# Laying the second memory's split and keys between other tiles, and four more seven-product tiles, in a decoder trunk on one core

## The chip, the cores and the metric

The kernel runs on one core of a Trainium2 chip. A core has a matrix engine (TensorE, PE in the profile, with its weight loads as PEld), a vector engine (VectorE, DVE), an activation engine (ScalarE, ACT), a general engine (GpSimd, POOL) and SyncE (SP), which here issues almost all DMAs. Each engine works through its own queue in order; engines wait for each other on semaphores. The metric is the time of one execution on the device in microseconds (us), as the median of several runs.

## The reference

The reference is a two-layer decoder trunk over 512 tokens of width 1024, all in float32:

```python
for layer in range(DEPTH):
    if layer % 2 == 0:
        x = x + even_mixer(rms_norm(x, ev_norm[j]), ...)   # pooling + latent attention
    else:
        x = x + odd_mixer(rms_norm(x, od_norm[j]), ...)    # conv, gates, linear scan
    x = x + mem_cross_attention(rms_norm(x, xa_norm_x[layer]), mem, xa_norm_mem[layer], ...)
    x = x + swiglu(rms_norm(x, ffn_norm[layer]), ffn_w_gate_up[layer], ffn_w_down[layer])
return rms_norm(x, final_norm)
```

The pieces that the change touches:

```python
def odd_mixer(h, ...):
    gate_branch, xb = jnp.split(h @ w_in, [LRU_WIDTH], axis=-1)
    xb = causal_depthwise_conv(xb, conv_w, conv_b)
    ...                                  # sigmoid gates r, i; a = exp(log_a); b = mult * (i * xb)
    _, hseq = lax.associative_scan(linear_scan_combine, (a, b), axis=1)
    return (jax.nn.gelu(gate_branch) * hseq) @ w_out

def mem_cross_attention(h, mem, norm_mem, w_q, w_kv, w_o):
    m = rms_norm(mem, norm_mem)          # 256 memory tokens
    k, v = jnp.split(m @ w_kv, 2, axis=-1)
    ...

def swiglu(h, w_gate_up, w_down):
    g, u = jnp.split(h @ w_gate_up, 2, axis=-1)
    return (jax.nn.silu(g) * u) @ w_down
```

## The kernel before, in words

**Layout and precision.** Activations lie transposed: 1024 features are eight tiles of 128 partitions, with the 512 tokens along the free axis. To keep float32 accuracy with a rounded matmul type, each operand is split into a high and a low part. ACT writes the high part (a rounding copy), DVE the difference. A product of two split operands takes three matmuls (`mm3`, L162 to L171: high times high, high times low, low times high). So a matmul row in the profile has the line L169, L170 or L171 wherever it is issued, and the name of the tile that it writes (`mm`, `att`, `s`, `tr`, the four pairs of result banks) tells the places apart. A split of an activation has the lines L156 and L157, or L159 and L160 where a gain is multiplied in.

**Weights** (`Weights.get`, L84) are loaded by SyncE into two buffers of up to 128 x 1024 (L93), and split by ACT (L101) and DVE (L102) into four buffers each for the high and the low part. All stages share these buffers, in the order in which their weights are called for.

**The FFN** (`ffn`, L762) has 22 hidden tiles, in parts of 4, 4, 4, 4 and 6. A plain tile (L863) makes gate and up products of 512 columns, 2 x 8 x 3 = 48 matmuls. A seven-product tile (`fast`, L811) treats the same 2 x 2 block product by the seven-product scheme: 7 x 4 x 3 = 84 matmuls of 256 columns. It needs sums of weight halves (`sa`, `sb`, DVE), its own splits (`sw_h`, `sw_l`), and combines the results on DVE. Its raw weights (`gr`, L815) and the combined activations (`ta`, `tb`) live in a pool that is open only for the FFN (`st`, L879). Each hidden tile is multiplied by Silu (L855 in a seven-product tile, L866 in a plain one) and split (`hidden`, L781). After each part but the last, the down projection of that part is run two output tiles at a time behind the hidden tiles of the next part (`todo`, L913). `FAST` (L36) says which hidden tiles take the seven-product form: its first entry is for the second FFN, its second for the first.

At the end of the first FFN, the last part's down projection gives eight output tiles (L925). Each is added to the residual (L278, DVE) and fed to the next norm: split with the next block's gain (L159, L160) and squared (`feed`, L259). After the second output tile `aside` is called (L927). It makes the memory's second copy, `mg`: eight tiles of 256 columns, each scaled and split (L365, so L159 on ACT and L160 on DVE).

At the end of the second FFN, the last part's down weights are kept whole for the tail (`tailh`, `taill`, L885), in a pool that opens where the seven-product pool was closed (L883), before the last part's six tiles.

**The recurrent block** (`odd`, L931). Four heads of convolution tiles (`conv_tile`, L966) and gate products (`odg`, L1015, banks `att`) feed Sigmoid and Tanh on ACT. Then come eight tiles of the Gelu branch (`gate_tile`, L1041): 24 matmuls of 512 columns in bank `mm`, read out by a DVE multiply (L1044). Then the keys of the second memory (`mem_keys`, L369): eight tiles, 24 matmuls of 256 columns each, same banks, read out by L378. Then the scan (L1025: Exp and Square on ACT, L1031, L1035 and the scan instruction L1036 on DVE, with Sqrt on ACT between). Then Gelu of the eight gate tiles, their product with the scan's result (L1057) and its split, and the output projection (`odout`).

**What sets the order.** The program is written in one order, but a planner (the tile framework) lays each engine's queue: among the instructions that its own model has ready, it takes those earlier in the program first. It runs what is ready ahead of what still waits, across block borders. `issue_after(ins)` pins what follows behind `ins` in that engine's queue.

Of the kernel before, what the change touches and what calls it, by code (L numbers as in the profile page):

```python
# [9 lines left out]
F32 = mybir.dt.float32  # L10
F32R = mybir.dt.float32r
BF16 = mybir.dt.bfloat16
I32 = mybir.dt.int32
AF = mybir.ActivationFunctionType
ALU = mybir.AluOpType
# [3 lines left out]
P = 128  # L19
T = 512  # L20
D = 1024
KD = D // P
# [10 lines left out]
DFF = 2816  # L33
NF = DFF // P
FFN_PARTS = (4, 4, 4, 4, 6)
FAST = range(5, 16), range(5, 22)  # L36
HT = T // 2
KH = KD // 2
WARM = 12
# [67 lines left out]
class Trunk:  # L107
# [45 lines left out]
    def split(self, src, hi, lo, scale=None):  # L153
        nc = self.nc
        if scale is None:
            nc.scalar.copy(hi, src)  # L156
            nc.vector.tensor_sub(lo, src, hi.bitcast(F32))  # L157
        else:
            nc.scalar.activation(hi, src, AF.Copy, scale=scale)  # L159
            nc.vector.scalar_tensor_tensor(lo, src, scale, hi.bitcast(F32), op0=ALU.mult, op1=ALU.subtract)  # L160

    def mm3(self, out, terms, begin=True, end=True, **kw):  # L162

# [180 lines left out]
            self.nc.sync.dma_start(t, self.ins["memT"][i * 2 * P:(i + 1) * 2 * P, :].rearrange("(m p) t -> p m t", p=P))  # L344
        return [t[:, i, :] for t in tiles for i in range(2)]

    def mem_gained(self, layer, pool, tag, keys=True):


        nc = self.nc  # L350
        mem = self.mem_load(keys)
        mg = pool.tile([P, 2, KD, MEM], F32R, name=self.nm("mg"), tag=tag)
        if self.Rmem is None:
            ssq = self.new_ssq()
            for m in range(KD):
                self.add_square(ssq, mem[m], m == 0)
            cols = self.rstd_cols((ssq, D, NMT, None), bank="mm")[0]
            self.rmem = self.cst.tile([P, NMT], F32, name="rmem", tag="rmem")
            nc.vector.tensor_copy(self.rmem, cols)
            ps = self.bcast(cols, NMT, bank="mm")  # L360
            self.Rmem = self.cst.tile([P, MEM], F32, name="Rmem", tag="Rmem")
            nc.scalar.copy(self.Rmem, ps[:, :MEM])
        res = []
        for m in range(KD):
            self.split(mem[m], mg[:, 0, m, :], mg[:, 1, m, :], scale=self.vec("xa_norm_mem", layer * KD + m))  # L365
            res.append((mg[:, 0, m, :], mg[:, 1, m, :]))
        return res

    def mem_keys(self, layer, mg, m0, m1, low=None):  # L369

# [391 lines left out]
    def ffn(self, layer, nrm, nxt_spec, aside=None):  # L762


        nc, ins, tc = self.nc, self.ins, self.tc
        xg, A = nrm["xg"], nrm["side"]
        B = 1 - A
        final = nxt_spec is None
# [5 lines left out]
        lo, hi = slice(0, HT), slice(HT, T)  # L774
        xn, TA, TB = [None] * KD, [], []

        def products(f, xs):
            pg = self.linear(Wg, (layer * NF + f) * 2, xs, bank="mm")
            return pg, self.linear(Wg, (layer * NF + f) * 2 + 1, xs, bank="att")

        def hidden(u):  # L781
            h, l = self.pair(A)
            self.split(u, h, l)
            return h, l
# [78 lines left out]
        def plain(f):  # L863
            pg, pu = products(f, xn)
            t, u = self.tmp("t0"), self.tmp("t1")
            nc.scalar.activation(t, pg, AF.Silu)  # L866
            nc.vector.tensor_mul(u, pu, t)
            return hidden(u)
# [8 lines left out]
        todo, f0, nxt = [], 0, None  # L877
        fastp = ExitStack()
        st = fastp.enter_context(self.tc.tile_pool(name=f"fast{layer}", bufs=1))  # L879
        for p, nf in enumerate(FFN_PARTS):  # L880
            last = p == len(FFN_PARTS) - 1
            if last and final:
                fastp.close()  # L883
                pool = self.ctx.enter_context(self.tc.tile_pool(name="tail", bufs=1))
                into = [pool.tile([P, KD, nf * P], F32R, name=f"tail{i}", tag=f"tail{i}") for i in "hl"]  # L885
                Wd = Weights(self, ins[f"ffn_down{p}"], f"dn{layer}_{p}", into=into)
            hs = []
            if p == 0:

                pg = self.linear(Wg, layer * NF * 2, xg, bank="mm")  # L890
                with tc.issue_after(self.mm_ins):
                    cols = self.rstd_cols((nrm["ssq"], D, NT, None))[0]
                with tc.issue_after(self.sum_ins):
                    ps = [(pg, self.linear(Wg, layer * NF * 2 + 1, xg, bank="att"))]
                with tc.issue_after(self.mm_ins):
                    row = self.bcast(cols)
                R = self.rp.tile([P, T], F32, name=self.nm("R"), tag="R")
                nc.scalar.copy(R, row)
                with tc.issue_after(self.row_ins):
                    ps.append(products(1, xg))  # L900
                for i, (pg, pu) in enumerate(ps):
                    t, u = self.tmp("t0"), self.tmp("t1")
                    nc.vector.tensor_mul(t, pg, R)
                    nc.scalar.activation(t, t, AF.Silu)
                    nc.vector.tensor_mul(u, pu, R)
                    nc.vector.tensor_mul(u, u, t)
                    if i == 0:
                        gs = normed(st)
                    hs.append(hidden(u))
                halves(st, gs)  # L910
            for f in range(f0 + len(hs), f0 + nf):
                hs.append(fast(f, st) if f in FAST[not final] else plain(f))
                for _ in range(2):  # L913
                    if todo:
                        m = KD - len(todo)
                        self.residual(m, todo.pop(0)())
            f0 += nf
            if not last:
                todo = down(p, hs)
        if final:  # L920
            self.tail(Wd, hs, layer * KD, B)
# [2 lines left out]
        nxt = self.next_norm(B, *nxt_spec)  # L924
        for m, run in enumerate(down(p, hs)):  # L925
            self.residual(m, run(), nxt)
            if m == 1 and aside:  # L927
                aside()
        return nxt

    def odd(self, nrm, nxt_spec):  # L931
        nc, ins, tc = self.nc, self.ins, self.tc
# [5 lines left out]
        with ExitStack() as ctx:  # L938
            pool = ctx.enter_context(tc.tile_pool(name="od", bufs=1))
# [101 lines left out]
            def gate_tile(m):  # L1041
                ps = self.linear(Win, m, xg)
                t = self.actp.tile([P, T], F32, name=self.nm("g"), tag=f"act{other}")
                nc.vector.tensor_mul(t, ps, self.Rrow)  # L1044
                return t
# [1 line left out]
            self.Rrow = self.norm_row(nrm["ssq"], D)  # L1047
            sums, row = self.sum_ins, self.row_ins
            lru_gates()
            gates = [gate_tile(m) for m in range(KD)]  # L1050
            self.mem_keys(1, self.mg, 0, KD, None)
            lru_scan()
            with run():
                for m, t in enumerate(gates):
# [83 lines left out]
@with_exitstack  # L1138
def tile_trunk(ctx: ExitStack, tc: tile.TileContext, ins, out):
    k = Trunk(ctx, tc, ins, out)  # L1140
    nrm = k.setup()
    nrm = k.even(nrm, ("xa_norm_x", 0))
    nrm = k.cross(0, nrm, ("ffn_norm", 0))
    with ExitStack() as kept:
        def ready():
            k.mg = k.mem_gained(1, kept.enter_context(tc.tile_pool(name="mg1", bufs=1)), "mg")

        nrm = k.ffn(0, nrm, ("od_norm", 0), ready)
        nrm = k.odd(nrm, ("xa_norm_x", KD))
        nrm = k.cross(1, nrm, ("ffn_norm", KD), k.mg)  # L1150
    k.ffn(1, nrm, None)
# [82 lines left out]
```

## Time and profile before

| | |
|---|---|
| median of 3 runs | 1397.79 us (1396.98 to 1399.87) |
| profiled execution, its own time | 1396.59 us |
| its span, first to last instruction | 1394.8 us |
| TensorE busy | 1359.9 us, 97% |
| weight loads busy | 1178.4 us, 84% |
| VectorE busy | 927.0 us, 66% |
| ScalarE busy | 655.1 us, 47% |
| GpSimd busy | 122.0 us, 9% |
| bytes read from memory | 135.93 MB |
| mean granted clock | 0.992 |

The profile is of one execution. A row of a group or of the order in time names the line of the kernel, the engine, the operation and its tiles as out<-in. Time in square brackets is how long the engine was idle before the instruction, with the one that released it. The granted clock is the share of full speed that the chip's throttle gave TensorE in that stretch. Matmuls overlap, so one matmul's duration is longer than the distance to the next.

### The profile page before, as it was taken

The page shows a single profiled execution, that of the slowest core. Times are in us where ns is not written, and L with a number is a line of the kernel's source. Part 1 is how long each engine was busy: PE and PEld are TensorE (multiplying, and loading weights), DVE is VectorE, ACT ScalarE, POOL GpSimd, SP SyncE. Part 2 cuts the span into 40 slices and gives each one's busy share as a digit, 9 for nine tenths or more (in the row PEclk, how much of TensorE's full clock was granted, in tenths as well). Part 3 has the DMA queues.
Part 4 walks back from the last instruction along what each step waited for, and adds up shares of the span by engine and source line. Part 5 has one row for each costly group of instructions (what it writes and reads, how often), then busy time and mean ns, then how long its engine had stood idle before and what let it go on. Part 6 is the DMA issues. An engine that isn't in the chain of part 4 may idle for free.

```text
span 1394.8 us, 19076 instructions
## 1 busy us (share of the span) xinstructions
PE 1359.9 (97%) x7496; PEld 1178.4 (84%) x7496; DVE 927.0 (66%) x1449; ACT 655.1 (47%) x1053; POOL 122.0 (9%) x131
## 2 busy tenths in 40 slices
PE   8989999999999999999899979999999999999997
PEld 7777788888889999999788868888888999998887
DVE  6787574455787777777778595435549777764443
ACT  6577653354444444444535664335435344443231
POOL 0441021013000000000110001211120000000001
PEclk9999999999999999999999999999999999999999
DMA  6331252223242323331322324222324223213231
GB/s 208 99 97 39 75 183 89 93 89 105 82 141 96 107 91 109 103 103 31 115 96 90 106 79 163 91 76 91 106 95 145 93 95 103 94 53 125 92 91 61
DMA packets 44970, 139.40 MB, mean 100 GB/s; under 512 B 5584, under 2 KB 9808, under 8 KB 44880
## 3 DMA queue, kind: packets, MB, share of 16 engines
q1 hardware_dynamic: 43440, 136.86, 30.2%
q8 instruction: 59, 0.97, 0.3%
q10 hardware_dynamic: 1440, 1.32, 0.3%
q14 instruction: 31, 0.25, 0.1%
HBM read 135.93 MB, written 2.10 MB: 99 GB/s over the span
## 4 chain that ended last, share of the span: by engine, by line
PE 87%; DVE 5%; ACT 3%; issue 2%; DMA 0%; POOL 0%; POOLq 0%; DVEq 0%; ACTq 0%
PE mm L169 14%; PE mm L170 14%; PE mm L171 14%; PE s L171 6%; PE s L170 6%; PE s L169 6%; PE att L169 6%; PE att L170 6%; PE att L171 6%; PE tr L170 1%; PE tr L171 1%; PE tr L169 1%; DVE xk_l L102 1%; DVE act L157 1%; PE att L680 1%
## 5 line engine op out<-in xcount | busy, mean ns | idle before, releaser
L169 PE MATMUL s<-act,dn_h 128*128 128x512 f32 x304 | 120.0, 395 | 3.2 <-ACT act L156 3.2
L170 PE MATMUL s<-act,dn_h 128*128 128x512 f32 x304 | 120.0, 395 | 0.6 <-DVE act L157 0.6
L171 PE MATMUL s<-act,dn_l 128*128 128x512 f32 x304 | 116.3, 396 | 0.0
L250 POOL TENSOR_TENSOR ssq<-ssq,t 128x512 f32<-128x512 f32 (+1 forms) x37 | 59.1, 1598 | 633.4 <-ACT t L249 633.1
L156 ACT CAST sw_h<-gr 128x1024 fp32r<-128x1024 f32 (+1 forms) x56 | 46.8, 835 | 92.9 <-PE att L170 52.6
L278 DVE TENSOR_TENSOR x<-s,x 128x512 f32<-128x512 f32 x72 | 49.6, 688 | 35.8 <-PE s L171 35.7
L101 ACT CAST gu_h<-gu_raw 128x1024 fp32r<-128x1024 f32 x32 | 33.7, 1053 | 83.5 <-PE mm L170 53.1
L169 PEld LDWEIGHTS s<-act,dn_h 128*128 128x128 f32 x304 | 57.8, 190 | 14.7 <-ACT act L156 3.7
L170 PEld LDWEIGHTS s<-act,dn_h 128*128 128x128 f32 x304 | 57.9, 190 | 11.7 <-DVE act L157 1.0
L171 PEld LDWEIGHTS s<-act,dn_l 128*128 128x128 f32 x304 | 57.9, 190 | 10.4
L157 DVE TENSOR_TENSOR sw_l<-gr,sw_h 128x1024 fp32r<-128x1024 f32 (+1 forms) x56 | 53.6, 957 | 14.8 <-ACT sw_h L156 12.1
L170 PE MATMUL mm<-tb,sw_h 128*128 128x256 f32 x224 | 63.4, 283 | 0.0
L171 PE MATMUL mm<-tb,sw_l 128*128 128x256 f32 x224 | 63.3, 283 | 0.0
L169 PE MATMUL mm<-tb,sw_h 128*128 128x256 f32 x224 | 62.8, 280 | 0.0
L101 ACT CAST dn_h<-dn_raw 128x1024 fp32r<-128x1024 f32 (+1 forms) x40 | 40.3, 1007 | 46.2 <-ACT pc L846 14.6
L156 ACT CAST sw_h<-sb 128x1024 fp32r<-128x1024 f32 x28 | 29.4, 1048 | 65.8 <-PE s L170 58.2
L102 DVE TENSOR_TENSOR dn_l<-dn_raw,dn_h 128x1024 fp32r<-128x1024 f32 (+1 forms) x40 | 46.8, 1171 | 14.5 <-ACT dn_h L101 14.1
L102 DVE TENSOR_TENSOR gu_l<-gu_raw,gu_h 128x1024 fp32r<-128x1024 f32 x32 | 39.2, 1224 | 23.3 <-ACT gu_h L101 23.2
L278 DVE TENSOR_TENSOR x<-mm,x 128x512 f32<-128x512 f32 x24 | 16.4, 691 | 51.7 <-PE mm L171 51.7
L169 PE MATMUL mm<-act,gu_h 128*128 128x512 f32 x128 | 50.6, 395 | 0.0
L171 PE MATMUL mm<-act,xq_l 128*128 128x512 f32 x128 | 50.1, 391 | 0.0
L169 PE MATMUL att<-act,gu_h 128*128 128x512 f32 x128 | 50.0, 390 | 0.0
(478 smaller groups left out, 4450.7 us busy)
## 6 DMA issues: line engine op xcount, KB each, us to landing
gr<-in_ffn_gu_dram SPq DMA_DIRECT2D x56, 512.0 KB, 3.5
gu_raw<-in_ffn_gu_dram SPq DMA_DIRECT2D x32, 512.0 KB, 3.5
dn_raw<-in_ffn_down_dram SPq DMA_DIRECT2D x32, 512.0 KB, 3.5
xk_raw<-in_xa_w_k_dram SPq DMA_DIRECT2D x16, 512.0 KB, 3.5
xq_raw<-in_xa_w_q_dram SPq DMA_DIRECT2D x16, 512.0 KB, 3.5
xv_raw<-in_xa_w_v_dram SPq DMA_DIRECT2D x16, 512.0 KB, 3.5
xo_raw<-in_xa_w_o_dram SPq DMA_DIRECT2D x16, 512.0 KB, 3.5
odin_raw<-in_od_w_in_dram SPq DMA_DIRECT2D x16, 512.0 KB, 3.5
```

The costliest lines, as they stand in the source:

```text
L101: nc.scalar.copy(hi, src)
L102: self.low.tensor_sub(lo, src, hi[:, :].bitcast(F32))
L156: nc.scalar.copy(hi, src)
L157: nc.vector.tensor_sub(lo, src, hi.bitcast(F32))
L169: nc.tensor.matmul(out, wh, xh, start=begin and i == 0, stop=False, **kw)
L170: nc.tensor.matmul(out, wh, xl, start=False, stop=False, **kw)
L171: self.mm_ins = nc.tensor.matmul(out, wl, xh, start=False, stop=end and i == last, **kw).ins
L250: (low or nc.gpsimd).tensor_add(ssq[:, :n], ssq[:, :n], sq[:, :n])
L278: self.nc.vector.tensor_add(self.x[m], ps, self.x[m] if src is None else src)
L680: nc.tensor.matmul(banks[t], a[:, ts], wh[:, ws], start=k == 0, stop=False)
```

## The change

Three edits. In the second FFN, hidden tiles 16 to 19 take the seven-product form; the seven-product pool is therefore closed, and the tail's pool opened, before tile 20 instead of before tile 16. The split of the memory's second copy is made in pieces, and after output tiles 1 to 7 of the first FFN one or two of them are queued behind that tile's own split, on ACT and on DVE. In the recurrent block, keys 0 to 3 follow gate tiles 0 to 3, and keys 4 to 7 follow gate tiles 4 to 7.

```diff
-FAST = range(5, 16), range(5, 22)
+FAST = range(5, 20), range(5, 22)
@@ def split
-            nc.scalar.copy(hi, src)
-            nc.vector.tensor_sub(lo, src, hi.bitcast(F32))
+            a = nc.scalar.copy(hi, src)
+            b = nc.vector.tensor_sub(lo, src, hi.bitcast(F32))
...
+        self.split_ins = a.ins, b.ins
@@ def mem_gained(..., later=False)
-        res = []
-        for m in range(KD):
+        def piece(m):
             self.split(mem[m], mg[:, 0, m, :], mg[:, 1, m, :], scale=self.vec("xa_norm_mem", layer * KD + m))
-            res.append((mg[:, 0, m, :], mg[:, 1, m, :]))
-        return res
+            return mg[:, 0, m, :], mg[:, 1, m, :]
+
+        return piece if later else [piece(m) for m in range(KD)]
@@ def ffn
-            last = p == len(FFN_PARTS) - 1
-            if last and final:
-                fastp.close()
-                pool = self.ctx.enter_context(self.tc.tile_pool(name="tail", bufs=1))
-                into = ...
-                Wd = ...
...
             for f in range(f0 + len(hs), f0 + nf):
+                if final and f == FAST[0].stop:
+                    fastp.close()
+                    pool = self.ctx.enter_context(tc.tile_pool(name="tail", bufs=1))
+                    into = ...
+                    Wd = ...
                 hs.append(fast(f, st) if f in FAST[not final] else plain(f))
...
         for m, run in enumerate(down(p, hs)):
             self.residual(m, run(), nxt)
-            if m == 1 and aside:
-                aside()
+            if aside:
+                a, b = self.split_ins
+                with tc.issue_after(a), tc.issue_after(b):
+                    aside(m)
@@ def odd
-            gates = [gate_tile(m) for m in range(KD)]
-            self.mem_keys(1, self.mg, 0, KD, None)
+            gates = []
+            for m in (0, KH):
+                gates += [gate_tile(i) for i in range(m, m + KH)]
+                self.mem_keys(1, self.mg, m, m + KH)
             lru_scan()
@@ def tile_trunk
-        def ready():
-            k.mg = k.mem_gained(1, kept.enter_context(tc.tile_pool(name="mg1", bufs=1)), "mg")
+        def ready(m):
+            if m == 0:
+                k.mg = []
+                k.piece = k.mem_gained(1, kept.enter_context(tc.tile_pool(name="mg1", bufs=1)), "mg", later=True)
+            k.mg += [k.piece(i) for i in ((), (0,), (1, 2), (3,), (4,), (5,), (6,), (7,))[m]]
```

More of the change, by code (lines that the diff above doesn't have):

```diff
@@ L155, in split @@
         if scale is None:
-            nc.scalar.copy(hi, src)
-            nc.vector.tensor_sub(lo, src, hi.bitcast(F32))
-        else:
-            nc.scalar.activation(hi, src, AF.Copy, scale=scale)
-            nc.vector.scalar_tensor_tensor(lo, src, scale, hi.bitcast(F32), op0=ALU.mult, op1=ALU.subtract)
+            a = nc.scalar.copy(hi, src)
+            b = nc.vector.tensor_sub(lo, src, hi.bitcast(F32))
+        else:
+            a = nc.scalar.activation(hi, src, AF.Copy, scale=scale)
+            b = nc.vector.scalar_tensor_tensor(lo, src, scale, hi.bitcast(F32), op0=ALU.mult, op1=ALU.subtract)
+        self.split_ins = a.ins, b.ins
     def mm3(self, out, terms, begin=True, end=True, **kw):
@@ L345, in mem_load, with mem_gained @@
         return [t[:, i, :] for t in tiles for i in range(2)]
-    def mem_gained(self, layer, pool, tag, keys=True):
+    def mem_gained(self, layer, pool, tag, keys=True, later=False):
         nc = self.nc
@@ L880, in ffn @@
         for p, nf in enumerate(FFN_PARTS):
-            last = p == len(FFN_PARTS) - 1
-            if last and final:
-                fastp.close()
-                pool = self.ctx.enter_context(self.tc.tile_pool(name="tail", bufs=1))
-                into = [pool.tile([P, KD, nf * P], F32R, name=f"tail{i}", tag=f"tail{i}") for i in "hl"]
-                Wd = Weights(self, ins[f"ffn_down{p}"], f"dn{layer}_{p}", into=into)
             hs = []
@@ L911, in ffn @@
             for f in range(f0 + len(hs), f0 + nf):
+                if final and f == FAST[0].stop:
+                    fastp.close()
+                    pool = self.ctx.enter_context(tc.tile_pool(name="tail", bufs=1))
+                    into = [pool.tile([P, KD, nf * P], F32R, name=f"tail{i}", tag=f"tail{i}") for i in "hl"]
+                    Wd = Weights(self, ins[f"ffn_down{p}"], f"dn{layer}_{p}", into=into)
                 hs.append(fast(f, st) if f in FAST[not final] else plain(f))
@@ L917, in ffn @@
             f0 += nf
-            if not last:
+            if f0 < NF:
                 todo = down(p, hs)
```

## The prediction

> **What bounds the kernel now.** I read the page first, then the waits of TensorE, then the busy time of the engines in chosen stretches, and last the instructions in order of time around the two places that these views point to.
>
> ```profile
> span 1394.8 us, 19076 instructions
> PE 1359.9 (97%) x7496; PEld 1178.4 (84%) x7496; DVE 927.0 (66%) x1449; ACT 655.1 (47%) x1053; POOL 122.0 (9%) x131
> ```
>
> TensorE (PE) bounds the kernel: it is idle for 35 us of 1394.8. So there are two ways to gain: fewer matmuls, or less of those 35 us. The profiled execution took 1396.59 us, 1.8 more than its span, and lies 1.2 below the median of 1397.79; every sum below is taken from 1396.59, and 1.2 is added for the median.
>
> Waits of PE over the whole span; the columns are total us, times, longest:
>
> ```profile
> PE mm L169 <- DVE g L1044: 6.8, 2, 6.2
> PE s L169 <- ACT act L156: 3.2, 1, 3.2
> ...
> PE mm L169 <- DVE keys L378: 0.8, 1, 0.8
> ...
> PE s L170 <- DVE act L157: 0.6, 1, 0.6
> ```
>
> Two places hold most of it: the end of the first FFN (3.2 + 0.6) and the gates and keys of the recurrent block (6.8 + 0.8). The change touches both. Busy time by stretch (length, then PE, PEld, DVE, ACT, POOL, then the granted clock):
>
> ```profile
> 675.81:682.64 6.83, 6.39 (x14) 4.65 (x15) 6.40 (x16) 4.65 (x8) 1.38 (x1) 0.50 0.31 73
> ...
> 819.60:822.59 2.99, 0.06 (x1) 0.00 (x0) 2.99 (x5) 2.14 (x4) 0.00 (x0) 1.00 0.24 99
> 822.59:829.41 6.82, 3.52 (x16) 3.55 (x17) 6.82 (x11) 4.01 (x7) 0.00 (x0) 0.50 0.12 34
> 829.41:834.25 4.84, 4.03 (x35) 3.86 (x33) 4.84 (x9) 1.67 (x2) 0.00 (x0) 1.00 0.49 173
> 834.25:848.70 14.45, 14.45 (x120) 14.45 (x121) 10.40 (x18) 7.49 (x12) 0.00 (x0) 1.00 0.51 161
> ...
> 805.00:820.00 15.00, 14.07 (x72) 11.35 (x70) 15.00 (x19) 9.91 (x15) 0.00 (x0) 1.00 0.30 98
> ```
>
> After each of the two waits the granted clock is 0.50 for 6.8 us. The busy matmul time inside counts half: 6.39 / 2 = 3.2 us are lost at the first place, 3.52 / 2 = 1.8 at the second. So the first place costs 3.2 + 0.6 + 3.2 = 7.0 us, the second 6.8 + 0.8 + 1.8 = 9.4. Note also that VectorE (DVE) has no idle time at all from 805 to 834.25: in that stage it, not PE, sets the pace.
>
> **Part one: four more seven-product tiles (f = 16 to 19 of the second FFN).** A plain tile issues 48 matmuls of 512 columns, a seven-product tile 84 of 256. Each tile calls Silu once, so the distance between two Silus is the time of one tile with its two output tiles. L855 is the seven-product tile, L866 the plain one; the last two rows are the last product's read-out at today's boundary and the first cast into the tail's weights:
>
> ```profile
> 1241.29 0.63 ACT L855 ACTIVATE t<-t 128x512 f32<-128x512 f32 x1
> ...
> 1256.87 0.63 ACT L855 ACTIVATE t<-t 128x512 f32<-128x512 f32 x1
> ...
> 1302.38 0.59 ACT L866 ACTIVATE t<-mm 128x512 f32<-128x512 f32 x1
> ...
> 1318.70 0.59 ACT L866 ACTIVATE t<-mm 128x512 f32<-128x512 f32 x1
> ...
> 1328.48 0.84 ACT L101 CAST tailh<-dn_raw 128x768 fp32r<-128x768 f32 x1 [3.70 <-DMA dn_raw<-in_ffn_down_dram]
> ```
> ```profile
> 1265.07 0.42 DVE L859 SCALAR_TENSOR_TENSOR t<-mm,t 128x256 f32<-128x256 f32 x1 [0.90 <-PE mm L171]
> ```
>
> 15.58 against 16.32: 0.74 us per tile, **3.0 us** for four. The extra work (sums of weights, smaller casts, two combinations per tile) falls on DVE and ScalarE (ACT), and PE covers it:
>
> ```profile
> 1120.00:1155.00 35.00, 35.00 (x243) 32.69 (x242) 27.33 (x38) 14.94 (x21) 0.00 (x0) 1.00 0.29 99
> ...
> 1295.00:1330.00 35.00, 35.00 (x156) 28.97 (x156) 13.87 (x16) 9.91 (x12) 0.00 (x0) 1.00 0.29 97
> ```
>
> In the seven-product stage DVE is at 27.33 of 35 and PE still at 35.00; were that cover gone, DVE's 12 us per tile would be the next bound, still under 15.58. The eight weight loads of these tiles move from the two-buffer weight pool to the tiles' own buffers. What moves later is the opening of the tail's weight space, which lies where the seven-product tiles' buffers were. Today the last such tile reads out 8.2 us after its Silu (1265.07 - 1256.87); four tiles on, that is 1256.87 + 4 x 15.58 + 8.2 = 1327.4, and the tail's first cast is at 1328.48 already. So it is hidden by 1 us, and behind that by the two plain tiles that stay. Bounds: 0 if the casts come late enough to cost it all, 3.0 as measured. I take 3.0.
>
> **Part two: the memory's split laid among the first FFN's output tiles.** ACT, then DVE, in order of time:
>
> ```profile
> 670.25 0.84 ACT L101 CAST dn_h<-dn_raw 128x768 fp32r<-128x768 f32 x1 [5.32 <-PE mm L170]
> 670.99 3.30 ACT L159 ACTIVATE mg<-keys,vecs 128x256 fp32r<-128x256 f32 x8
> ...
> 674.29 0.60 ACT L156 CAST act<-t 128x512 fp32r<-128x512 f32 x1
> 674.91 1.28 ACT L950 ACT_TABLE_LOAD   x1
> ```
> ```profile
> 671.12 0.96 DVE L102 TENSOR_TENSOR dn_l<-dn_raw,dn_h 128x768 fp32r<-128x768 f32 x1
> ...
> 672.33 3.25 DVE L160 SCALAR_TENSOR_TENSOR mg<-keys,vecs,mg 128x256 fp32r<-128x256 f32 x8
> 675.49 0.69 DVE L157 TENSOR_TENSOR act<-t,act 128x512 fp32r<-128x512 f32 x1
> ...
> 677.09 0.17 DVE L954 TENSOR_TENSOR sp_z<-sp_z 128x8 f32<-128x8 f32 x1
> ```
>
> The split of the last hidden tile, for which PE waits, stands in both queues behind all eight pieces of the memory: 3.2 us on each engine. Pinned behind the output tiles' own splits, the pieces can no longer get ahead of it. ACT's cast then starts near 671.1 and DVE's difference near 675.49 - 3.16 = 672.3. What is late next is that difference: PE's second product waits until about 673, some 0.9 us, and the first output tiles' read-out perhaps 0.6 more. Of 7.0 us, 1.5 stay: a gain of **5.5**, if the clock keeps up. The rows ask for about 3 us of idle before a drop (2.99 before 822.59, 3.2 here); 1 to 1.5 us is well under.
>
> [...]
>
> The pieces themselves: one per output tile (0.49 on ACT, 0.48 on DVE). One output tile on DVE:
>
> ```profile
> 692.90 0.69 DVE L278 TENSOR_TENSOR x<-s,x 128x512 f32<-128x512 f32 x1 [1.81 <-PE s L171]
> 693.76 1.23 DVE L102 TENSOR_TENSOR odin_l<-odin_raw,odin_h 128x1024 fp32r<-128x1024 f32 x1 [0.17 <-ACT odin_h L101]
> 694.90 0.75 DVE L160 SCALAR_TENSOR_TENSOR act<-x,vecs,act 128x512 fp32r<-128x512 f32 x1
> ```
>
> 2.7 of some 4 us, so half a microsecond more costs nothing; what queues behind a piece is the next tile's weight split, which is early. The memory's own load is not on this path:
>
> ```profile
> L344 SPq DMA_DIRECT2D keys<-in_memT_dram x8: 379/448/680, 8.2 to 180.6; - x8
> ```
>
> Its last transfer is issued at 180.6. Bounds: 0 to 7.0; a loss is excluded, since nothing new is put ahead of the split.
>
> **Part three: four key tiles between the gate tiles.** Nothing is added or removed; eight gate tiles (24 matmuls of 512) and eight key tiles (24 of 256) change order, and with them the weight loads on SyncE's queue and their splits. DVE, with two rows of PE:
>
> ```profile
> 805.36 1.20 DVE L102 TENSOR_TENSOR xk_l<-xk_raw,xk_h 128x1024 fp32r<-128x1024 f32 x1
> ...
> 815.79 0.66 DVE L1044 TENSOR_TENSOR g<-mm,R 128x512 f32<-128x512 f32 x1
> ...
> 825.08 0.67 DVE L1044 TENSOR_TENSOR g<-mm,R 128x512 f32<-128x512 f32 x1
> ...
> 826.26 1.22 DVE L102 TENSOR_TENSOR xk_l<-xk_raw,xk_h 128x1024 fp32r<-128x1024 f32 x1
> ...
> 835.48 0.68 DVE L157 TENSOR_TENSOR act<-h,act 128x512 fp32r<-128x512 f32 x1
> ...
> 839.85 1.23 DVE L102 TENSOR_TENSOR xk_l<-xk_raw,xk_h 128x1024 fp32r<-128x1024 f32 x1 [1.21 <-ACT xk_h L101]
> ```
> ```profile
> 816.16 0.39 PE L171 MATMUL mm<-act,odin_l 128*128 128x512 f32 x1
> ...
> 848.71 0.40 PE L169 MATMUL mm<-act,odout_h 128*128 128x512 f32 x1
> ```
>
> The last gate tile's matmuls end at 816.55, its read-out comes at 825.08: 8.5 us in DVE's queue behind the scan. It holds one of two banks, so PE waits. The eight key weights are ready between 806.6 and 841.1, one per 4.9 us, because their splits stand in the same queue; a key tile needs only 24 x 14.45 / 120 = 2.9 us of PE. In the new order the first four keys use weights that are split before 800, where gate weights are split today, and the late slots serve gates 4 to 7 (24 x 35 / 156 = 5.4 us of PE each, more than 4.9) and keys 4 to 7. DVE's work is the same, so its last slot, 841.1, stays; key 7 follows with 2.9 us and the output projection starts at 844.0 instead of 848.71: 4.7. As the gate tiles now arrive later, DVE has fewer of their products to do around 820 and the slots come a little sooner: I take **5.0**. Bounds: 9.4 if PE never waits; on the other side, if each of four key tiles is read out 8.5 us late, two banks make one tile per (2.9 + 8.5) / 2 = 5.7 us, 2.8 more than now, 11.2 in all, with 3.2 for a clock drop: 9.4 - 14.4, a loss of 5.
>
> **Sum:** 3.0 + 5.5 + 5.0 = 13.5; 1396.59 - 13.5 + 1.2 = 1384.3, say **1384**.
>
> **Rivals.** *A: the FFN stall is refilled.* With the pieces gone, ACT's table load (1.28) and DVE's row of some twenty small instructions (0.17 to 0.2 each, 4 us) may slip ahead of the hidden tile's split as the pieces did. For: they already stand directly behind it. Against: they depend on one another and on the table, so they become ready one by one. Then 1 of 5.5 is left: gain 9.0, 1389.
>
> *B: DVE keeps the odd stage.* It is busy without a gap there, no work is taken from it, and the instruction order in its queue is the planner's; if the halves come out in an order that leaves PE waiting as long as now, part three gives 0: gain 8.5, 1389. That the change does not do what it says (the keys still queued behind all gates) gives the same. A and B together leave 4: 1394.
>
> *C: slower.* Gate 7 moves from before the keys to their middle. Its way to the output projection (read-out, Gelu, product, split) took from 816.55 to 836.16, 20 us. Its weight is now ready at 827.5, its matmuls end at 832.9, and after the same 20 us its product is there at 853. The projection starts at 844 and can run 21 of 24 matmuls of two tiles without it, 42 x 0.224 = 9.4 us, to 853.4: just covered. From 20.5 us on, each microsecond costs one, and 3.2 more for the clock; the gain is eaten at 31 us. If each of the three DVE steps waits as long again, 40 us, PE waits 19.5 + 3.2 and the time is 1384 + 22.7 = 1407. For: the queue is saturated. Against: DVE's backlog ends near 841.
>
> **Chances.** Forecast 0.48, A 0.15, B 0.20, both 0.07, C 0.10. The likeliest alone spans 1379 to 1388, just short of A and B. The range for 8 in 10 runs from 1377 (3.0 + 7.0 + 9.4 = 19.4, the whole of both places, and 1.4 for the spread of the runs) to 1396, which takes in A, B and both; C lies outside. A measurement of this kernel can tell about 0.2%, 2.8 us: faster takes forecast, A, B and part of both, 0.80; same 0.09; slower 0.11.
>
> **What would show it.** Silus of f = 16 to 19 at 15.6 us (part one), and the tail's first matmul without a wait. No group of eight pieces before the last hidden split, PE's wait there near 1 us, granted clock 1.00 through 675 to 683 (part two). PE's wait for the gate read-out under 2 us in total, clock 1.00 around 822, the output projection starting 4 to 5 us sooner relative to the start of the stage (part three). Wrong if PE waits for small instructions of the next block (A), for key or gate read-outs as long as now (B), or in the projection for the last product (C).

## The result, and the profile after

The changed kernel takes **1384.64 us** (1382.47 to 1386.88) where the kernel before, timed beside it, takes 1398.49 (1396.98 to 1399.87): a ratio of 0.9906, 95% interval 0.9892 to 0.9920. In a second session it took 1386.82 beside 1397.67, ratio 0.9917 (0.9899 to 0.9936). Its profiled execution took 1385.45 us, 11.1 less than the one before. The head of its page:

```profile
span 1383.7 us, 19425 instructions
...
PE 1353.7 (98%) x7640; PEld 1180.2 (85%) x7640; DVE 951.2 (69%) x1489; ACT 665.8 (48%) x1073; POOL 121.9 (9%) x131
```

TensorE (PE) is busy for 6.2 us less and idle for 30 us in place of 35. PE's waits at the two places, from the waits of the whole span and of the stretch around the first FFN's end (total us, times, longest):

```profile
PE mm L170 <- DVE g L1046: 2.8, 1, 2.8
...
PE mm L170 <- DVE keys L379: 2.3, 2, 1.6
...
PE s L171 <- DVE act L157: 0.6, 1, 0.6
PE s L170 <- DVE x L279: 0.5, 1, 0.5
```

The code's lines have moved by a few: the gate read-out is L1046, the keys' L379, the product L1061, the matmuls L170 to L172. The stall at the FFN's end is down to 0.6 + 0.5. Of 7.6 us at the gates and keys, 5.1 are left. Where the time went is read from starts in the order of time. The changed kernel:

```profile
670.05 0.28 PE L172 MATMUL mm<-tb,sw_l 128*128 128x256 f32 x1
...
704.79 0.39 PE L187 MATMUL tr<-ones,ssq 128*128 128x1 f32 x3
...
782.90 1.28 ACT L987 ACT_TABLE_LOAD   x1
...
840.47 0.39 PE L170 MATMUL mm<-act,odout_h 128*128 128x512 f32 x1
...
1339.21 0.34 PE L170 MATMUL mm<-act,tailh 128*128 128x384 f32 x1
```

The kernel before:

```profile
670.05 0.28 PE L171 MATMUL mm<-tb,sw_l 128*128 128x256 f32 x1
...
710.38 0.50 PE L186 MATMUL tr<-ones,ssq 128*128 128x1 f32 x4
...
788.49 1.28 ACT L985 ACT_TABLE_LOAD   x1
...
1350.37 0.34 PE L169 MATMUL mm<-act,tailh 128*128 128x384 f32 x1
```

The five rows are the last seven-product matmul of the first FFN, the sum for the next norm, the scan's first table load, the output projection (848.71 before) and the tail. Up to 670.05 the two traces take the same time. The distances to the next row hold one part each: 34.74 against 40.33 us at the end of the FFN (part two, 5.6), 57.57 against 60.22 from the table load to the projection (part three, 2.65), 498.74 against 501.66 from there to the tail (part one, 2.9). From the norm's sum to the table load both take 78.11.

Part one, in ScalarE's (ACT) order; the four new seven-product tiles lie between the first two rows:

```profile
1248.65 0.62 ACT L856 ACTIVATE t<-t 128x512 f32<-128x512 f32 x1
...
1310.99 0.63 ACT L856 ACTIVATE t<-t 128x512 f32<-128x512 f32 x1
1321.41 0.84 ACT L101 CAST tailh<-dn_raw 128x768 fp32r<-128x768 f32 x1 [0.77 <-DMA dn_raw<-in_ffn_down_dram]
```

The distance is 62.34 / 4 = 15.585 us per tile. Part two, first ACT, then VectorE (DVE), with the clock behind it (length; busy time of PE, PEld, DVE, ACT, POOL; granted clock):

```profile
671.11 0.60 ACT L156 CAST act<-t 128x512 fp32r<-128x512 f32 x1
671.73 1.28 ACT L952 ACT_TABLE_LOAD   x1
...
672.34 0.68 DVE L157 TENSOR_TENSOR act<-t,act 128x512 fp32r<-128x512 f32 x1
```
```profile
675.81:682.64 6.83, 6.83 (x32) 5.65 (x31) 6.83 (x15) 5.37 (x11) 1.73 (x2) 1.00 0.37 115
```

The last hidden tile's split stands ahead of the table load and of every piece of the memory, and the clock stays at 1.00 where it was 0.50. Part three, DVE's queue with the matmul that waits for it, and the last matmul of gate 5:

```profile
813.98 0.67 DVE L1037 TENSOR_TENSOR i<-h,i 128x512 f32<-128x512 f32 x1
814.57 1.22 DVE L1038 TENSOR_TENSOR_SCAN h<-r,i 128x512 f32<-128x512 f32 x1
815.70 2.47 DVE L1061 TENSOR_TENSOR h<-g,h 128x512 f32<-128x512 f32 x4
818.09 1.22 DVE L102 TENSOR_TENSOR xk_l<-xk_raw,xk_h 128x1024 fp32r<-128x1024 f32 x1
819.23 0.68 DVE L1061 TENSOR_TENSOR h<-g,h 128x512 f32<-128x512 f32 x1
819.83 1.22 DVE L1038 TENSOR_TENSOR_SCAN h<-r,i 128x512 f32<-128x512 f32 x1
820.96 0.66 DVE L1046 TENSOR_TENSOR g<-mm,R 128x512 f32<-128x512 f32 x1
...
829.15 0.69 DVE L1046 TENSOR_TENSOR g<-mm,R 128x512 f32<-128x512 f32 x1 [3.46 <-PE mm L172]
830.05 1.23 DVE L102 TENSOR_TENSOR xk_l<-xk_raw,xk_h 128x1024 fp32r<-128x1024 f32 x1 [0.21 <-ACT xk_h L101]
```
```profile
813.14 0.39 PE L172 MATMUL mm<-act,odin_l 128*128 128x512 f32 x1
...
821.77 0.47 PE L170 MATMUL mm<-act,odin_h 128*128 128x512 f32 x1 [2.80 <-DVE g L1046]
```

Gate 5's matmuls end at 813.5. Its read-out starts at 820.96, 7.4 us later, behind two scans (one with a product of its own, L1037), five products of gate and scan (L1061) and a weight split. Gate 7 needs its bank, so PE waits. And then DVE itself waits 3.46 us for PE's gate 7, with the last key weight's split queued behind that read-out.

### The profile page after: what moved, and what is told of

It reads as the page before. It is cut to its first block, busy times and chain, and to the rows that moved or that the text cites. A ratio compares the mean times of both kernels' runs of the same rounds, so it can differ in the third digit from the quotient of the medians.

```text
span 1383.7 us, 19425 instructions
## 1 busy us (share of the span) xinstructions
PE 1353.7 (98%) x7640; PEld 1180.2 (85%) x7640; DVE 951.2 (69%) x1489; ACT 665.8 (48%) x1073; POOL 121.9 (9%) x131
## 4 chain that ended last, share of the span: by engine, by line
PE 87%; DVE 5%; ACT 3%; issue 2%; DMA 0%; POOL 0%; POOLq 0%; DVEq 0%; ACTq 0%
PE mm L170 14%; PE mm L171 14%; PE mm L172 14%; PE s L172 6%; PE s L170 6%; PE s L171 6%; PE att L170 6%; PE att L171 6%; PE att L172 6%; PE tr L171 1%; PE tr L172 1%; PE tr L170 1%; PE att L681 1%; DVE h L1038 1%; PE mm L683 1%
## 5 line engine op out<-in xcount | busy, mean ns | idle before, releaser
L170 PE MATMUL s<-act,dn_h 128*128 128x512 f32 x304 | 119.2, 393 | 0.5 <-DVE x L279 0.5
L172 PE MATMUL s<-act,dn_l 128*128 128x512 f32 x304 | 114.6, 393 | 0.0
L156 ACT CAST sw_h<-gr 128x1024 fp32r<-128x1024 f32 x64 | 53.4, 835 | 106.3 <-PE att L171 58.7
L157 DVE TENSOR_TENSOR sw_l<-gr,sw_h 128x1024 fp32r<-128x1024 f32 x64 | 61.3, 958 | 17.7 <-ACT sw_h L156 14.6
L171 PE MATMUL mm<-tb,sw_h 128*128 128x256 f32 x256 | 72.5, 283 | 0.0
L172 PE MATMUL mm<-tb,sw_l 128*128 128x256 f32 x256 | 72.3, 283 | 0.0
L170 PE MATMUL mm<-tb,sw_h 128*128 128x256 f32 x256 | 71.8, 280 | 0.0
L156 ACT CAST sw_h<-sb 128x1024 fp32r<-128x1024 f32 x32 | 33.6, 1049 | 75.4 <-PE s L171 67.8
L170 PEld LDWEIGHTS s<-act,dn_h 128*128 128x128 f32 x304 | 57.3, 189 | 11.3 <-DVE x L279 0.9
L172 PEld LDWEIGHTS s<-act,dn_l 128*128 128x128 f32 x304 | 57.2, 188 | 10.0
L101 ACT CAST gu_h<-gu_raw 128x1024 fp32r<-128x1024 f32 x24 | 25.3, 1053 | 55.3 <-PE mm L171 37.7
L156 ACT CAST sw_h<-sa 128x1024 fp32r<-128x1024 f32 x32 | 33.6, 1050 | 34.5 <-PE mm L171 33.0
L172 PE MATMUL mm<-act,xq_l 128*128 128x512 f32 x128 | 50.1, 391 | 0.0
L171 PE MATMUL mm<-act,xq_h 128*128 128x512 f32 x128 | 50.0, 390 | 0.0
L170 PE MATMUL mm<-act,xq_h 128*128 128x512 f32 x128 | 49.9, 390 | 0.0
```

What stands on the lines that cost most here:

```text
L156: a = nc.scalar.copy(hi, src)
L157: b = nc.vector.tensor_sub(lo, src, hi.bitcast(F32))
L170: nc.tensor.matmul(out, wh, xh, start=begin and i == 0, stop=False, **kw)
L171: nc.tensor.matmul(out, wh, xl, start=False, stop=False, **kw)
L172: self.mm_ins = nc.tensor.matmul(out, wl, xh, start=False, stop=end and i == last, **kw).ins
```

## The experiments

**The parts alone.** Each of three kernels has one part of the change.

```diff
 part one alone: after, without the other two
-                with tc.issue_after(a), tc.issue_after(b):
-                    aside(m)
+                aside(m)
...
-            k.mg += [k.piece(i) for i in ((), (0,), (1, 2), (3,), (4,), (5,), (6,), (7,))[m]]
+            k.mg += [k.piece(i) for i in ((), tuple(range(KD)), (), (), (), (), (), ())[m]]
...
+            gates = [gate_tile(m) for m in range(KD)]
+            self.mem_keys(1, self.mg, 0, KD, None)
 part two alone: this order of gates and keys, and FAST as before
 part three alone: the first two of these, and FAST as before
```

> Part one alone: four more fast tiles in the second FFN, the memory's split and keys as before. My theory: the three parts stand at three places of the kernel and add up, so this one gives what the changed kernel's trace shows between the output projection and the tail's first matmul, 2.9 us: about 1395 us, a ratio near 0.998 to the kernel before. The rival, that the parts help each other, makes the three single gains sum to clearly less than the 11 us between the two profiles; this one would then be 0 to 2 us.

> Part two alone: the eight pieces of the memory's split laid one by one behind output tiles of the first FFN. My theory: 5.6 us, the shift of the first Exp table load in the changed kernel's trace (788.49 to 782.90 us), so about 1392 us and a ratio near 0.996; the keys' phase is as long as before, 60.2 us from that table load to the output projection (788.49 to 848.71). The rival, that the parts help each other: another length of the keys' phase with the split out of its way, and a gain away from 5.6 us by over 1 us.

> Part three alone: four keys between the gate tiles, with the split where it was. My theory: about 2.7 us (the output projection came 8.2 us earlier in the changed kernel and the table load before it only 5.6), so about 1395 us and a ratio near 0.998, with VectorE's read-out of gate 5 again behind four products and TensorE waiting some 2.8 us for it. The rival, the prediction's own term: 5.0 us, about 1392.5 us, which part two's earlier start of the stage took away in the changed kernel.

Measured: part one 1394.77 us, 0.9975 (0.9963 to 0.9988) of the kernel before; part two 1393.58, 0.9964 (0.9946 to 0.9981); part three 1395.74, 0.9987 (0.9971 to 1.0003). In us that is 3.5, 5.0 and 1.8, together 10.3, each uncertain by some 2; the interval of part three still holds no change at all. The traces say it more sharply. Distances between the five rows, and between the last of them and the end, in us, for every kernel that ran (the last seven are explained below; in brackets, for 1 to 2 and 3 to 4, the stretch at half clock inside that distance, from the clock's record):

| kernel | start to row 1 | 1 to 2 | 2 to 3 | 3 to 4 | 4 to 5 | 5 to end |
|---|---|---|---|---|---|---|
| before | 670.05 | 40.33 (6.83) | 78.11 | 60.22 (6.83) | 501.66 | 44.44 |
| changed | 670.05 | 34.74 | 78.11 | 57.57 (3.41) | 498.74 | 44.45 |
| changed, again | 671.06 | 34.71 | 78.11 | 55.92 | 498.79 | 44.43 |
| part one alone | 671.82 | 38.85 (3.41) | 78.11 | 60.22 (6.83) | 498.71 | 44.44 |
| part two alone | 674.00 | 34.77 | 78.11 | 60.23 (6.83) | 501.69 | 44.44 |
| part three alone | 674.68 | 40.87 (6.83) | 78.11 | 58.78 (6.83) | 501.67 | 44.44 |
| pieces not held | 670.01 | 40.89 (6.83) | 78.11 | 58.83 (6.83) | 498.74 | 44.46 |
| pieces at once | 673.18 | 34.93 | 78.11 | 55.96 | 498.77 | 44.45 |
| products behind gate 5 | 672.12 | 34.75 | 78.11 | 54.01 | 498.87 | 44.44 |
| four banks for keys | 671.44 | 34.77 | 78.11 | 52.55 | 498.70 | 44.45 |
| both | 671.82 | 34.71 | 78.11 | 51.60 | 498.75 | 44.44 |
| both, again | 670.31 | 34.73 | 78.11 | 51.59 | 498.73 | 44.44 |
| gates last | 670.70 | 34.77 | 78.11 | 63.27 (6.83) | 499.90 | 44.44 |

Each part moves its own column, and the other columns differ only by the clock's drops and up to 0.6 us around one of them, so the parts add up; the rival of parts that help each other falls. Part one gives 2.8 to 3.0 in every kernel that has it but the last, whose column 4 to 5 also holds a wait in the projection. Part two gives 4.1 to 6.2 and part three 1.4 to 4.3, and what they give depends on the stretch at half clock, not on the other parts.

**What the half clock costs.** The same waits, 2.8 us before gate 7 and 2.3 at the keys, stand in five of these traces, with three lengths of column 3 to 4. Busy time and clock in successive windows of 3.41 us around the 2.8 us wait, first of the changed kernel's first trace, then of part three alone, then of the changed kernel's second trace:

```profile
819.21:822.62 3.41, 0.85 (x4) 0.74 (x5) 3.41 (x5) 0.63 (x1) 0.00 (x0) 1.00 0.45 154
822.62:826.03 3.41, 3.41 (x10) 2.64 (x9) 3.08 (x5) 1.58 (x2) 0.00 (x0) 0.50 0.47 154
826.03:829.45 3.42, 3.42 (x19) 2.87 (x18) 0.30 (x1) 0.48 (x1) 0.00 (x0) 1.00 0.48 153
```
```profile
828.37:831.78 3.41, 1.36 (x7) 0.79 (x5) 3.41 (x5) 0.00 (x0) 0.00 (x0) 1.00 0.15 40
831.78:835.20 3.42, 2.66 (x6) 2.15 (x7) 3.39 (x6) 2.16 (x3) 0.00 (x0) 0.50 0.45 147
835.20:838.61 3.41, 3.41 (x9) 2.64 (x8) 1.38 (x2) 0.05 (x1) 0.00 (x0) 0.50 0.70 261
```
```profile
817.65:821.06 3.41, 2.29 (x11) 1.56 (x9) 3.41 (x6) 0.26 (x1) 0.00 (x0) 1.00 0.00 0
821.06:824.48 3.42, 1.72 (x8) 1.47 (x9) 3.42 (x5) 1.25 (x2) 0.00 (x0) 1.00 0.46 153
824.48:827.89 3.41, 3.41 (x17) 2.83 (x16) 2.29 (x3) 0.96 (x2) 0.00 (x0) 1.00 0.56 189
```

In the trace of the kernel before, the clock's record has drops that start at 68.24, 675.81 and 822.59, which is 178 and then 43 times 3.413 us apart; each lasts 6.83. In the changed kernel's first trace they start at 68.27 and 822.62, 221 times 3.413 apart, and last 6.83 and 3.41. Their place against the kernel differs between executions: behind the scan's first table load, the drop at this wait starts after 39.7 us in the changed kernel (822.62 less 782.90) and after 38.1 in part three alone (831.78 less 793.66), where the wait itself starts after 36.1 in both (818.97 and 829.73). In the windows above, one with 2.56 or 2.05 us of idle PE is followed by one at half clock; those with 1.12 and 1.70 in the changed kernel's second trace are not. The half-clock window that still has 0.76 idle is followed by a second; those in which PE is busy throughout end the drop. So one and the same wait costs here a further 3.41 / 2 = 1.7 us, (2.66 + 3.41) / 2 = 3.0 us, or nothing. That fits column 3 to 4: take 5.1 and the clock's loss away from 57.57, 58.78 and 55.92, and 50.8, 50.7 and 50.8 are left.

So the 2.8 us wait cost clock in three of the five traces. Split over two windows (1.12 and 1.70) it cost nothing; 2.05 us of idle inside one window were enough.

All windows of 3.413 us in the two traces of the kernel before and of the changed one, laid by their own drops, from 6.8 us on, where the clock's record begins: at full clock, the seven with 1.85 to 3.41 us of idle PE (two of them at the kernel's end) were followed by half clock, and none of those with up to 1.70 was. Of the half-clock windows inside the kernel, the four with 0.43 us or more of idle (0.43, 1.51 twice, 3.31) were followed by another, the five with 0.25 or less were not. But idle time in the profile is not the whole measure. In the trace of "both, again", a window near 39 us has no idle PE time, and half clock follows:

```profile
39.14:42.55 3.41, 3.41 (x27) 3.19 (x27) 2.14 (x5) 1.05 (x1) 0.10 (x1) 1.00 0.22 78
42.55:45.96 3.41, 3.41 (x10) 2.63 (x9) 1.66 (x10) 0.00 (x0) 1.54 (x1) 0.50 0.24 77
```
```profile
L187 PE MATMUL tr<-ones,t 128*128 128x1 f32 x21 | 2.5, 250 | 0.0
```

The last row is a group of matmuls of the first window: 21 matmuls of a single column make up 2.5 of its 3.41 us. In the kernel before, such a group (22 matmuls, 2.5 us from 40.28 on) lies across the border of two windows at 40.94, and the clock stays at 1.00. Why the one window was followed by half clock was not tested.

**Is it the hold, or the laying out one by one?** Two kernels take part two apart.

```diff
 pieces not held in the queues behind the output tiles' splits
-                with tc.issue_after(a), tc.issue_after(b):
-                    aside(m)
+                aside(m)
 pieces held, but all at once after output tile 1
-            k.mg += [k.piece(i) for i in ((), (0,), (1, 2), (3,), (4,), (5,), (6,), (7,))[m]]
+            k.mg += [k.piece(i) for i in ((), tuple(range(KD)), (), (), (), (), (), ())[m]]
```

> The changed kernel with the memory's pieces written one by one among the output tiles as there, but not held behind them in the queues. Theory: the hold is what counts; without it the pieces of VectorE and ScalarE go ahead of the last hidden tile's split again, TensorE waits over 3 us there as before the change, and all 5.6 us of part two are lost: about 1390 us, ratio to the kernel before 0.9945 or so. The rival: writing the pieces at later places of the program is enough, the time stays at 1384.6 us within 1 us.

> The changed kernel with all eight pieces written after output tile 1 and held behind its read-out, not one by one. Theory: only their place behind the last hidden tile's split matters, the laying out one by one brings nothing: within 1 us of the changed kernel, 1384.6 us. The rival: eight pieces together (some 0.35 us each on either engine, 2.8 us) hold up the output tiles' read-outs and TensorE waits again by 1 to 3 us: 1386 to 1388 us.

Measured: 1390.80 us without the hold (0.9937, 0.9912 to 0.9961) and 1386.23 at once (0.9908, 0.9888 to 0.9928). Without the hold, ACT's order and PE's wait are those of the kernel before:

```profile
670.95 3.29 ACT L159 ACTIVATE mg<-keys,vecs 128x256 fp32r<-128x256 f32 x8
...
674.25 0.60 ACT L156 CAST act<-t 128x512 fp32r<-128x512 f32 x1
```
```profile
PE s L170 <- ACT act L156: 3.2, 1, 3.2
```

Held all at once, the median is 1.6 above the changed kernel's 1384.64, in the range that the rival named. But the rival's wait is not there: PE's waits at the end of the FFN are the 0.6 and 0.5 of the changed kernel, and column 1 to 2 is 34.93, 0.2 above it. That trace was late before this place, with row 1 at 673.18; where the other runs lost the 1.6 stays open. So the hold behind the output tiles gives part two but for those 0.2. Writing the pieces at later places of the program does nothing by itself: the planner takes whatever is ready, and all eight pieces are.

**Is it VectorE's pace, or its order?** The prediction said that DVE sets the pace of part three's stage. Two edits leave DVE's work as it is. One puts its eight products behind the read-out of gate 5. The other gives the keys four result banks of their own, so that keys and gates no longer wait for each other's read-outs. A third kernel has both.

```diff
 the products behind gate 5's read-out (gread: the read-outs, as gate_tile makes them)
-                nc.vector.tensor_mul(hs[m], t, hs[m])
+                with self.tc.issue_after(gread[5]):
+                    nc.vector.tensor_mul(hs[m], t, hs[m])
 four banks for the second memory's keys
-            ps = self.bank("mm")
+            ps = self.bank(("att", "s")[m % 2] if layer else "mm")
```

> The changed kernel with one order more: VectorE's eight products of gate and scan may be issued only behind the read-out of gate 5. Theory: the queue's order made the 2.8 us wait before gate 7; the read-out of gate 5 then ends about 3 us earlier (near 818 instead of 820.96 us), the wait falls under 1 us, and with it the clock's drop of 3.4 us (1.7 us of work lost) behind it: 3 to 4.5 us faster than the changed kernel, about 1380.5 to 1382 us where that one takes 1384.6, ratio to the kernel before near 0.988. The rival, the prediction's words that VectorE itself sets the pace there: the same VectorE work stands in another order, the wait appears at another gate or key, and the time is within 1 us of the changed kernel's.

> The changed kernel with four PSUM banks of their own for the second memory's keys, in place of the two which they share with the gate tiles. Theory: the 2.3 us that TensorE waits for the read-outs of keys 1 and 2 go, since no key and no gate then needs a bank that a key holds; the 2.8 us before gate 7 go too if the read-out of gate 5 comes before the four products now, and shrink to about 1 us if it still stands behind them: 3 to 6 us faster than the changed kernel with the clock's drop, 1379 to 1382 us. The rival, that VectorE sets the pace of the whole stage: TensorE waits as long at another place, no change over 1 us, 1384.6 us.

> Both: four banks for the keys, and VectorE's products of gate and scan behind the read-out of gate 5. Theory: the waits for keys (2.3 us) and for gate 5 (2.8 us) both go, and no drop of the clock follows: 2 us faster than with the order alone (1382.4 us), about 1380 us, ratio to the kernel before near 0.987; the stage from the first Exp table load to the output projection takes 51.5 to 52 us in place of 57.57. The rival, VectorE's pace: the wait comes back at the split of the key weights or at a read-out, and the time is that of the order alone within 1 us.

Measured: 1382.40 us (0.9889, 0.9874 to 0.9904), 1381.29 (0.9870, 0.9849 to 0.9891) and 1381.17 (0.9876, 0.9855 to 0.9896). The first is 2.2 us below the changed kernel's first median, where 3 to 4.5 were expected. The third is no faster than the second by the median; its column 3 to 4 is 1 us shorter. With the products behind it, gate 5's read-out comes straight after the scan, and the wait before gate 7 is gone; the keys' 2.3 us stay, and a new 0.7 us shows at a later key. DVE's queue and PE's waits of that kernel:

```profile
818.89 1.22 DVE L1038 TENSOR_TENSOR_SCAN h<-r,i 128x512 f32<-128x512 f32 x1
820.03 0.67 DVE L1046 TENSOR_TENSOR g<-mm,R 128x512 f32<-128x512 f32 x1
820.61 3.09 DVE L1062 TENSOR_TENSOR h<-g,h 128x512 f32<-128x512 f32 x5
```
```profile
PE mm L170 <- DVE keys L379: 2.3, 2, 1.6
PE mm L170 <- ACT act L156: 0.7, 1, 0.7
```

PE's waits in this stage with four banks alone, and then with both edits:

```profile
PE mm L170 <- DVE g L1046: 1.8, 2, 1.2
```

```profile
PE mm L170 <- DVE g L1046: 1.2, 1, 1.2
```

The same DVE work leaves PE waiting 5.1, 3.0, 1.8 or 1.2 us, and 50.8 plus these gives 55.9, 53.8, 52.6 and 52.0 against 55.9, 54.0, 52.6 and 51.6 measured where the clock did not drop. So the order and the banks made the waits. DVE's pace didn't, at least not down to 1.2 us; what the last 1.2 hang on was not tried.

**The changed kernel and the one with both edits, side by side.**

> The changed kernel itself, once more, beside the next one on the same chip. Theory: the spread of the runs (1382.5 to 1386.9 us before) comes from where idle stretches fall in the clock's 3.41 us windows: its profile shows the same 2.8 us and 2.3 us waits at the gates and keys, and the stage from the first Exp table load to the output projection takes one of three lengths, near 55.9 (no window at half clock), 57.6 (one) or 58.8 us (two). Time again 1384.6 us within 1 us. The rival: the waits themselves differ from run to run.

> Four banks for the keys and the products behind gate 5's read-out, once more, to compare with the changed kernel on one chip. Theory: 3.5 us faster than it (1381.2 against 1384.6), with runs that lie closer together in this stage, since no wait there is left that could drop the clock; the stage takes 51.6 us again. The rival: the difference of 3.5 us between two sessions was chance, and it is under 1.5 us here.

Measured: 1386.82 us (1384.82 to 1387.09) and 1380.48 (1379.72 to 1381.06), the latter 0.9876 (0.9856 to 0.9897) of the kernel before. The runs of the two do not overlap. The median of the changed kernel lies 2.2 above the earlier one, more than the 1 us that was expected; its trace shows the same waits, and the stage's length is one of the three forecast, 55.92. The kernel with both edits beats the other two: the changed one by 3.5 us in medians of different sessions and by 6.3 in the same session, where 3.5 were expected. Column 3 to 4 differs by 4.3 and 6.0 between their traces.

**What the four keys behind gate 7 cover.** All eight keys stand between gates 3 and 4, so that gate 7 is directly ahead of the output projection.

```diff
-            for m in (0, KH):
-                gates += [gate_tile(i) for i in range(m, m + KH)]
-                self.mem_keys(1, self.mg, m, m + KH)
+            gates += [gate_tile(i) for i in range(KH)]
+            self.mem_keys(1, self.mg, 0, KD)
+            gates += [gate_tile(i) for i in range(KH, KD)]
```

> The changed kernel with all eight keys between gates 3 and 4: gates 0 to 3, keys 0 to 7, gates 4 to 7, then the output projection at once. It measures what the four keys behind gate 7 cover. Theory: from the end of gate 7's matmuls to the last split product it took 11.3 us in the changed kernel (828.7 to 839.95), of which the projection's matmuls on the products that are there cover some 5 to 9: TensorE waits 2 to 6 us in the projection, with 0 to 3.4 us for the clock: 1388 to 1393 us. The rival, the prediction's 20 us for this way with 9.4 covered: 10.6 us of wait and 3.2 for the clock, 1398 us, no faster than the kernel before.

Measured: 1392.93 us, 0.9963 (0.9947 to 0.9978). PE's waits from the gates to the projection, then the projection's start and DVE's last splits:

```profile
PE mm L170 <- DVE keys L379: 7.6, 5, 3.3
...
PE mm L171 <- DVE act L157: 0.6, 1, 0.6
```
```profile
844.99 0.39 PE L172 MATMUL mm<-act,odin_l 128*128 128x512 f32 x1
846.85 0.73 PE L170 MATMUL mm<-act,odout_h 128*128 128x512 f32 x2 [1.47 <-ACT act L156]
...
848.65 4.30 DVE L157 TENSOR_TENSOR act<-h,act 128x512 fp32r<-128x512 f32 x7
```

From the end of gate 7's matmuls (845.4) to the last split (852.95) it is 7.6 us, not 20, and PE loses 1.5 + 0.6 = 2.1 in the projection. The time lies where the theory put it, but mostly for another reason: five waits for key read-outs, 7.6 us, and a drop of the clock by two windows (0.50 from 819.71 to 826.54).

## Why the prediction was right, point by point

**The bound** held: PE is the limit, and the time came from fewer matmul columns and fewer idle stretches at the two named places.

**Part one**, 3.0 us, measured 2.9. The distance of 15.58 per tile came out as 15.585. The forecast of 1327.4 for the last such tile's read-out, less the 8.2 us that the parts before save, is 1319.2, and the read-out stands at 1319.19. The tail's first cast follows at 1321.41, and PE has no wait from 1250 us to the end.

**Part two**, 5.5 us, measured 5.6. The difference was forecast for 672.3 and starts at 672.34; of the 1.5 us that were to stay, 0.6 + 0.5 did. Rival A fell: the table load stands behind the split, and the small instructions come one by one. The ground, "about 3 us of idle before a drop", was too generous: 2.05 in one window were enough in part three alone. The idle that is left here, 1.1 in all, is under that, and none of the nine traces with the hold shows a drop here; the least idle time ahead of a drop in the traces of the kernel before and of the changed one is 1.85, at 68 us. But in "both, again" a drop at 42.55 stands behind a window with none, so that 1.1 alone is no guarantee.

**Part three**, 5.0 us, measured 2.65 in the trace that was compared, and 1.4 to 4.3 over all: the term was mis-sized. The step that failed is "DVE's work is the same, so its last slot, 841.1, stays", with the remark that DVE sets the pace. The last key weight's split ends at 831.28, which is 48.4 us behind the stage's first table load, against 52.6 before (841.08 less 788.49): 4.2 us sooner, and DVE stood idle for 3.46 us shortly before it. Nor did the projection follow 2.9 us behind that split: it starts 9.2 us later, and from the start of gate 7 on PE runs that gate and the four keys up to the projection without a wait. In place of DVE's last slot stand the two things that the experiments changed: read-outs late in the queue behind products that nobody waited for yet, and two banks shared by gates and keys. The text had this in its lower bound, a tile read out 8.5 us late (7.4 here), but for four keys, not for one gate. Its sign, "under 2 us" of wait for the gate read-out, is wrong with 2.8. The rest of the miss is the clock: the text asked for 1.00 around 822 and put no drop into the sum, but 5.1 us of waits stayed, and they cost none, one or two windows at half clock. Of the 2.35 us missed in the compared trace, 0.7 are waits (the trace without a drop gains 4.3 of the 5.0) and 1.7 the drop.

**Rival B** had the mechanism that occurred, the planner's order, and half of its size. **Rival C** did not: in the changed kernel the last split ends at about 840, before the projection starts, and with the cover taken away its way is 7.6 us and the loss 2.1.

**The sum** was 13.5, and the two profiled executions differ by 11.1: the whole gap is part three's. The medians differ by 13.9 in the first session and 10.9 in the second, so that 1384 met the first median to 0.6 us and the second to 2.8. The nearness of the first is partly luck. The spread has a visible source: in the table, the distances 2 to 3, 4 to 5 and 5 to end agree to 0.2 us, but for part one and for the last kernel's wait in the projection. The other three columns hold drops of the clock, the first among them, with 4.7 us between the lowest and the highest. One of the three latest starts of row 1, part two alone with 674.00, comes with two half-clock windows ahead of it, at 148.37 and 168.85; the kernel before and the changed kernel's first trace, both with 670.05, are at full clock from 75.1 us to row 1.

## What to carry to other kernels

Where a planner lays the queues, moving code to a later place may change nothing as long as the work is ready, as it did here (1390.80 us without the hold); a hold behind a named instruction does (1386.23 with all pieces at once). An engine that is busy without a gap need not be the bound (the same DVE work left PE waiting 5.1 us or 1.2): look at who waits for which of its instructions, and put the read-outs that free a bank ahead of products that nobody waits for yet. Price a stall as its own length plus what the clock may add (here 5.1 us, and 0, 1.7 or 3.0 for the clock), and compare stages between rows of the trace, not totals, when a few us decide.

## What the hardware showed that was not expected

A stall's price in clock was not fixed. The same 2.8 us of wait was followed by no window, one window or two windows of 3.41 us at half clock, 0, 1.7 or 3.0 us, with 2.56 or 2.05 us of its idle time in the window ahead of a drop, and with 1.12 and 1.70 in two windows where there was none. Before the change all three inner drops (at 68, 676 and 823 us) happened to be two windows long, 6.83 us, which had looked like a fixed length. In the traces of the kernel before and of the changed one, a drop went on where a window still held 0.43 us or more of idle PE, and ended where it held 0.25 or less. In the first 200 us, where PE is idle for 15.7 us in the kernel before (and for 0.4 in the 460 us behind them), the half-clock windows differ between executions of kernels that are the same up to there: one at 42.55 in "both, again", two at 148.37 and 168.85 in part two alone, none at these places in the kernel before and in the changed one. Row 1 starts at 670.0 to 674.7 us. That alone is a spread of 0.3% of the kernel, more than the smallest of the three parts.
